# First feed-forward of a hybrid attention and mLSTM network: output projection token-major with 512 weight columns, results transposed by TensorE

## The chip, the cores and the metric

One core of one Trainium2 chip runs the whole program. The metric is the device time of one execution in microseconds; the number of a kernel is the median of its runs. The engines are TensorE (PE: matmuls, with the weight loads PEld on a path of their own), VectorE (DVE), ScalarE (ACT), GpSimd (POOL) and SyncE (SP, which issues most DMAs). PE reads its operands from SBUF and writes PSUM, which has eight banks of 128 partitions by 512 fp32 columns.

## The reference

A network of two layers, 512 tokens, width 1024, feed-forward width 2816, all fp32:

```python
def swiglu(xn, w_in, w_out):
    gu = xn @ w_in
    return (jax.nn.silu(gu[..., :D_FF]) * gu[..., D_FF:]) @ w_out
...
    h = x
    for i in range(DEPTH):
        j = i // N_MIXERS
        if i % N_MIXERS == 0:
            h = h + dilated_attention_mixer(rms_norm(h, attn_norm[j]), positions,
                                            attn_w_in[j], attn_w_out[j])
        else:
            h = h + mlstm_mixer(rms_norm(h, mlstm_norm[j]), mlstm_w_in[j], mlstm_conv_w[j],
                                mlstm_conv_b[j], mlstm_ig_bias[j], mlstm_fg_bias[j],
                                mlstm_head_gain[j], mlstm_w_out[j])
        h = h + swiglu(rms_norm(h, ffn_norm[i]), ffn_w_in[i], ffn_w_out[i])
    return rms_norm(h, final_norm)
```

So the order is: attention, feed-forward 0, mLSTM, feed-forward 1, final norm. The change touches the last product of feed-forward 0 (`@ w_out`), the addition to `h`, and the norm and the first projection of the mLSTM mixer behind it.

## The kernel before

The residual `h` is held feature-major: eight tiles of 128 features by 512 tokens (`h0` to `h7`, after feed-forward 0 `hn0` to `hn7`). Every fp32 product is made as three products of rounded parts, hi·hi, hi·lo and lo·hi (`SPLITS`); a value is split by ACT (the high part, `_h`) and DVE (the rest, `_l`). A weight chunk is 128 partitions by 1024 fp32 values (512 KB), loaded by SP, and split by L210 (ACT) and L211 (DVE).

*The output projection* (`output_products`, L1371) multiplies 2816 hidden features by 1024 outputs for 512 tokens. Twenty of the 22 hidden chunks go through a Strassen-Winograd scheme with 2x2 blocks: token halves by hidden halves by output halves. That gives seven products P1 to P7, each in five units of 256 hidden features (`UNITS`), 35 unit-products in all; the last two chunks ("rest") are multiplied plainly, in two column halves `first` and `second`. A list written by hand (`order`, L1560) fixes the sequence; each item's weights and operands are prepared two items ahead (`AHEAD`). The last three items, P4_3, P4_4 and second_0 (`TAIL`), are not run in that order but tile by tile, so that the results become ready one after the other.

The two feed-forwards run it in two forms. In feed-forward 0 (`sums_of_rows` true) the weights are stationary, in blocks of 128x128, and 256 tokens move: `tile_mm` (L1609 to L1619), 24 matmuls of 256 columns to a unit-product. The results come out feature-major. P5's weights are sums of rows that are loaded apart (`load_first_sum`: ten loads by SP, ten more by POOL that add in flight, tiles `f0S`). Half results are copied from bank to bank by ACT (`copy_half`, L1635) and added to `h` by DVE (`add_sum`, L1640). In feed-forward 1 the activations are stationary and 512 weight columns move (L2023, L2089): 12 matmuls of 512 columns to a unit-product. Its results come out token-major, which the final output wants.

*The seam into the mLSTM.* `natural` (L1629, DVE) adds a finished bank to the old `h` and permutes the tokens, giving `hn`. `norm` (L1094) then splits each of the eight `hn` into `n_h` (ACT, L228) and `n_l` (DVE, L229) and sums their squares (`n2sq` by ACT, L380, `n2ssum` by DVE, L381). The sums over features are four small matmuls (`n2ss`, L1109), which are deferred: they are issued inside the projection of the first value columns (`project_tokens_wide`, L320, tiles `mv0`), behind the tile that `amid` names, before `(1, 1)`: the second chunk's second token block. DVE takes the reciprocal root from there (L1111, L340, L190 to L195), builds eight diagonal blocks (`n2dg`, L349), and PE spreads them over the partitions (`n2bc`, L355) after the gates' matmuls (L1730); DVE copies that to `n2rbc` (L356). The gate rows and everything behind the first q and k projection (`mqk`, L241) use it.

Each engine runs its instructions in the program's order as a scheduler laid it out; `issue_after` and `defer` move single pieces within that order.

Of the kernel before, what the change touches and what calls it, by code (L numbers as in the profile page):

```python
# [17 lines left out]
P = 128  # L18
# [54 lines left out]
def tile_hybrid_dilated_attn_mlstm(  # L73
# [1020 lines left out]
    def norm(key, k0, name, ssum=None, wait=1):  # L1094
        pair = x_tiles(name)
        add = None
        if ssum is None:
            ssum, add = squares_of(name)
        for k in range(KC):
            split_act(pair[0][k], pair[1][k], h[k], col(key, k0 + k))  # L1100
            if add is not None:
                add(k)
        v = npl.tile([P, TB], F32, tag="rs_v4", name=name + "v", bufs=2)
        box = {}

        def sums():
            sp = ps.tile([P, 512], F32, tag="t", name=name + "ss", bufs=1)
            for tb in range(TB):
                nc.tensor.matmul(sp[:, tb:tb + 1], ssum[:, tb * P:(tb + 1) * P], ones[:, 0:1],  # L1109
                                 start=True, stop=True)  # L1110
            nc.vector.tensor_copy(v, sp[:, :TB])  # L1111
# [259 lines left out]
    def output_products(layer, fp, wo, sums_of_rows):  # L1371
# [11 lines left out]
        ROWS = ({"P2": (1, 0), "P7": (1, 1), "P4": (1, 1)} if sums_of_rows else  # L1383
                {"P2": (1, 0), "P7": (0, 0), "P3": (1, 1)})
# [23 lines left out]
        first_sums = {}  # L1408

        def load_first_sum(u):  # L1410

            src = [weight_rows(hk * UNITS + u, 1) for hk in range(2)]
            place = (((npl, "sq", 2),) * 2, ((npl, "rbc", 1), (fp, "gu0", 3)), ((fp, "u2", 1), (fp, "v5", 1)),
                     ((fp, "gu1", 2),) * 2, ((fp, "gu0", 3),) * 2)[u]
            parts = [(p.tile([P, 1, 512], F32, tag=tg, name="f%dS1_%d" % (layer, u), bufs=bufs), slice(k, k + 1))
                     for k, (p, tg, bufs) in enumerate(place)]
            for t, ks in parts:
                nc.sync.dma_start(t, src[0][:, ks])
                nc.gpsimd.dma_start(t, src[1][:, ks], accum_op=ALU.add)  # L1419
            first_sums[u] = parts  # L1420

        def prepare_first_sum(u, own, nm):

            view = lambda t: t.rearrange("p (k n) -> p k n", k=2)
            hi = wp.tile([P, 1024], F32R, tag="whi", name=nm + "_h", bufs=W_BUFS)
            lo = wp.tile([P, 1024], F32R, tag="wlo", name=nm + "_l", bufs=W_BUFS)
            for t, ks in first_sums[u]:
                nc.scalar.activation(view(hi)[:, ks], t, AF.Copy)
                subtract(view(lo)[:, ks], t, view(hi)[:, ks].bitcast(F32))
            whl["P5", u] = view(hi), view(lo)  # L1430
            for t, ks in first_sums[u]:
                subtract(view(own)[:, ks], t, view(own)[:, ks])
            split_operand("P5", u, sums[u])

        def prepare_product(name, u):
# [21 lines left out]
            in_place = ("P1", "P6", "P3") if sums_of_rows else ("P1", "P5", "P6", "P4")  # L1457
            if sums_of_rows and name == "P5":
                prepare_first_sum(u, t, nm)
                return  # L1460
            raw = t if name in in_place else load(*ROWS[name])
            if sums_of_rows:

                if name == "P7":
                    nc.vector.tensor_tensor(raw, raw, t, op=ALU.add)
                    add_rows(t, 1, 0)


            elif name == "P7":
# [3 lines left out]
            if sums_of_rows and name == "P1":  # L1473

                for i in {0: (0,), 1: (1,), UNITS - 1: range(2, UNITS)}.get(u, ()):
                    load_first_sum(i)
            if sums_of_rows:
                if name == "P6":
                    negate(t)
            elif name in ("P1", "P5"):  # L1480
# [15 lines left out]
            elif name == "P6":  # L1496
                split_operand(name, u, half(u, 1))
                if sums_of_rows:
                    subtract(sums[u], half(u, 1), half(u, 0))
            elif name == "P7":  # L1500
                split_operand(name, u, sums[u])
            elif name == "P3":
                if not sums_of_rows:
                    subtract(half(u, 1), half(UNITS + u, 0), half(u, 1))
                split_operand(name, u, half(UNITS + u, 1) if sums_of_rows else half(u, 1))
            elif name == "P4":
                if sums_of_rows:
                    subtract(half(UNITS + u, 0), half(UNITS + u, 0), half(u, 1))
                split_operand(name, u, half(UNITS + u, 0 if sums_of_rows else 1))

        def prepare_rest(n, pi):
# [9 lines left out]
            if sums_of_rows and n == second:  # L1521

                view = lambda t: t.rearrange("p (k n) -> p k n", k=2)
                raw = fp.tile([P, 1024], F32, tag="t1", name=nm + "_w")
                nc.sync.dma_start(view(raw), weight_rows(pi, n))
                t = fp.tile([P, 2, 1024], F32R, tag="w8", name=nm + "_hl", bufs=2)
                hi, lo = t[:, 0], t[:, 1]
                nc.scalar.activation(hi, raw, AF.Copy)
                subtract(lo, raw, hi.bitcast(F32))
                whl[n, pi] = view(hi), view(lo)  # L1530
            elif n == second:
# [10 lines left out]
        def during(j, i):  # L1542
            u = j // 2 - (FC // 2 - UNITS)
            if i == 1 and 0 <= u < UNITS:
                p, tag, bufs = (fp, "sums", UNITS - 1) if u < UNITS - 1 else (npl, "ssum", 1)
                sums.append(p.tile([P, 2, HALF], F32, tag=tag, name="f%dS%d" % (layer, u), bufs=bufs))
                if sums_of_rows:
                    subtract(sums[u], half(u, 1), half(u, 0))
                else:
                    nc.vector.tensor_tensor(sums[u], half(u, 1), half(UNITS + u, 1), op=ALU.add)  # L1550
            if i == 4 and 0 <= u < UNITS:
                subtract(half(u, 1), *((half(UNITS + u, 1), sums[u]) if sums_of_rows else (sums[u], half(u, 0))))
# [24 lines left out]
        def work(product, plain, then):  # L1577

            for i, (kind, *key) in enumerate(items[:-TAIL]):
                prepare(i + AHEAD)  # L1580
                key = tuple(key)
                if not sums_of_rows and key == ("P7", UNITS - 1):
# [8 lines left out]
            for i in range(len(items) - TAIL + AHEAD, len(items) - (not sums_of_rows)):  # L1591
# [4 lines left out]

    pair, rbc, _, hook = norm("ffn", 0, "n1", ssum)
    with ExitStack() as fctx:
        fp = pool(fctx, "ffn0")
        hid, during, prepare, work = output_products(0, fp, ffn_w_out[0], True)  # L1600
# [3 lines left out]
        F = [[ps.tile([P, 512], F32, tag=tag, name="fo%d" % n, bufs=3 if tag == "acc" else 2 - (tag == "t"))  # L1604
              for tag in tags] for n, tags in enumerate((("s", "s", "acc", "acc"), ("o", "o", "acc", "t")))]
        ts = [slice(0, HALF), slice(HALF, SEQ)]
        target = {"P1": (0, 0), "P2": (0, 0), "P5": (0, 1), "P3": (0, 1), "P6": (1, 0), "P7": (1, 0), "P4": (1, 0)}

        def tile_mm(acc, m, b, w, fresh=False):  # L1609
            for k in range(2):  # L1610
                for a_, b_ in SPLITS:
                    nc.tensor.matmul(acc, w[a_][:, k, m * P:(m + 1) * P], b[b_][k],
                                     start=(fresh and k == 0 and (a_, b_) == SPLITS[0]),
                                     stop=(k == 1 and (a_, b_) == SPLITS[-1]), skip_group_check=True)

        def product(name, u, b, w):
            n, t = target[name]
            for m in range(4):
                tile_mm(F[n][m][:, ts[t]], m, b, w, name == "P1" and u == 0)  # L1619

        def plain(n, pi, b, w):
            for m in range(4):
                tile_mm(F[n][m], m, b, w)

        old, h = h, []
# [7 lines left out]
        def copy_half(t):  # L1633
            for m in range(4):
                nc.scalar.activation(F[1][m][:, ts[t]], F[0][m][:, ts[t]], AF.Copy)  # L1635

        def add_sum(n):
            for m in range(4):
                o = old[4 * n + m][:, ts[1]]
                nc.vector.tensor_tensor(o, F[1][m][:, ts[0]], o, op=ALU.add)  # L1640

        def first_tiles():
            for m in range(4):
                natural(m, F[0][m])
        last = work(product, plain, {("P1", 4): lambda: copy_half(0), ("P5", 4): lambda: copy_half(1),
                                     ("P6", 4): lambda: add_sum(0), ("P7", 4): lambda: add_sum(1)})
        first_tiles()

# [492 lines left out]
```

## Time and profile before

| | us |
|---|---|
| median of 3 runs | 1397.77 (1396.92 to 1398.39) |
| the profiled execution | 1398.66 |
| its span | 1396.7 |
| PE busy | 1380.6 |
| DVE busy | 1120.2 |
| ACT busy | 703.0 |
| POOL busy | 153.7 |

The span is the time between the first and the last instruction of the profiled execution, on which all times of the trace lie. An engine's busy time counts the time in which it had an instruction under way; matmuls overlap, so that a matmul's own duration in the trace is longer than the distance to the next one, and the pace is read from starts.

### The profile page before, as it was taken

What the parts mean: (1) busy time and instruction counts of PE and PEld (TensorE: products, weight loads), DVE (VectorE), ACT (ScalarE), POOL (GpSimd) and SP (SyncE); (2) the same over time, 40 slices, a digit from 0 to 9 for tenths busy, and PEclk for the clock granted to TensorE, in tenths of its full rate; (3) what the DMA queues carried; (4) which work ended last, traced back from release to release, by engine and by line L of the source; (5) the groups of instructions that cost most, each with busy time, mean ns of one, the idle gap of its engine ahead of it and who ended that gap; (6) DMA issues with size and microseconds to landing.
All of it is one profiled execution on the core that took longest, in us unless ns stands there. A gap on an engine that the chain in (4) does not pass through costs nothing. (4 is left out here: it accounts for less than half of the span.)

```text
span 1396.7 us, 21529 instructions
## 1 busy us (share of the span) xinstructions
PE 1380.6 (99%) x8308; PEld 1232.4 (88%) x8308; DVE 1120.2 (80%) x1904; ACT 703.0 (50%) x1153; POOL 153.7 (11%) x223
## 2 busy tenths in 40 slices
PE   9999999999999999999999999999999999999997
PEld 7888888888888788999999998888888899999886
DVE  7978769695868299877877898898858987887877
ACT  5335552222324155445566464786534544458854
POOL 1000011111010000000010100113201240001213
PEclk9999999999999999999999999999999999999999
DMA  7534256346363446333253643324334563335963
GB/s 228 164 121 136 76 166 190 120 138 195 96 191 92 157 145 158 121 122 115 92 164 85 154 134 92 92 77 106 95 117 116 134 196 121 122 104 133 198 162 106
DMA packets 136830, 186.00 MB, mean 133 GB/s; under 512 B 8532, under 2 KB 104340, under 8 KB 136728
## 3 DMA queue, kind: packets, MB, share of 16 engines
q1 hardware_dynamic: 117600, 136.14, 30.5%
q0 software_dynamic: 17472, 47.37, 14.7%
q8 instruction: 65, 1.06, 0.3%
q10 hardware_dynamic: 1656, 1.12, 0.2%
q14 instruction: 37, 0.30, 0.1%
HBM read 163.63 MB, written 18.87 MB: 131 GB/s over the span
## 5 line engine op out<-in xcount | busy, mean ns | idle before, releaser
L1444 POOL DMA_DIRECT2D f1T<-in_ffn_w_out_dram x15 | 17.8, 1186 | 207.5 <-DMA f1P_2w_w<-in_ffn_w_out_dram 136.0
L1419 POOL DMA_DIRECT2D f0S<-in_ffn_w_out_dram x10 | 8.8, 919 | 256.7 <-DMA f0S<-in_ffn_w_out_dram 189.6
L1976 POOL DMA_DIRECT2D hD<-hB x32 | 21.7, 697 | 68.5 <-DVE hB L1973 68.2
L241 PE MATMUL mo<-n_h,mo_k_l 128*128 128x512 f32 x64 | 25.3, 396 | 0.0
L241 PE MATMUL mo<-n_h,mo_k_h 128*128 128x512 f32 x64 | 25.2, 394 | 0.0
L241 PE MATMUL mo<-n_l,mo_k_h 128*128 128x512 f32 x64 | 25.2, 393 | 0.0
L241 PE MATMUL mqk<-n_h,mqk_k_h 128*128 128x512 f32 x64 | 25.1, 393 | 0.0
L241 PE MATMUL mwo<-yo_l,mwo_k_h 128*128 128x512 f32 x64 | 25.1, 392 | 0.0
L241 PE MATMUL awo<-ao_h,awo_k_h 128*128 128x512 f32 x64 | 25.1, 392 | 0.0
L241 PE MATMUL mqk<-n_l,mqk_k_h 128*128 128x512 f32 x64 | 25.1, 392 | 0.0
L241 PE MATMUL f0j<-n_h,f0j_h 128*128 128x512 f32 x64 | 25.0, 391 | 0.0
L241 PE MATMUL f1j<-n_h,f1j_h 128*128 128x512 f32 x64 | 25.0, 391 | 0.0
L241 PE MATMUL mwo<-yo_h,mwo_k_l 128*128 128x512 f32 x64 | 25.0, 391 | 0.0
L241 PE MATMUL mqk<-n_h,mqk_k_l 128*128 128x512 f32 x64 | 25.0, 390 | 0.0
L241 PE MATMUL awo<-ao_h,awo_k_l 128*128 128x512 f32 x64 | 24.9, 390 | 0.0
L241 PE MATMUL f0j<-n_h,f0j_l 128*128 128x512 f32 x64 | 24.9, 390 | 0.0
L241 PE MATMUL f1j<-n_h,f1j_l 128*128 128x512 f32 x64 | 24.9, 390 | 0.0
L241 PE MATMUL awo<-ao_l,awo_k_h 128*128 128x512 f32 x64 | 24.9, 389 | 0.0
L241 PE MATMUL f0j<-n_l,f0j_h 128*128 128x512 f32 x64 | 24.9, 389 | 0.0
L241 PE MATMUL f1j<-n_l,f1j_h 128*128 128x512 f32 x64 | 24.9, 389 | 0.0
L241 PE MATMUL mwo<-yo_h,mwo_k_h 128*128 128x512 f32 x64 | 24.8, 391 | 0.0
L211 DVE TENSOR_TENSOR v1P_l<-v1W,v1P_h 128x1024 fp32r<-128x1024 f32 x14 | 17.1, 1223 | 9.6 <-ACT v1P_h L210 9.6
(2491 smaller groups left out, 5671.1 us busy)
## 6 DMA issues: line engine op xcount, KB each, us to landing
f0j_w<-in_ffn_w_in_dram SPq DMA_DIRECT2D x17, 512.0 KB, 6.0
f1j_w<-in_ffn_w_in_dram SPq DMA_DIRECT2D x17, 512.0 KB, 5.4
f1T<-in_ffn_w_out_dram POOLq DMA_DIRECT2D x15, 512.0 KB, 6.7
f0hid<-in_ffn_w_in_dram SPq DMA_DIRECT2D x9, 512.0 KB, 5.5
f1hid<-in_ffn_w_in_dram SPq DMA_DIRECT2D x9, 512.0 KB, 5.0
v0W<-in_attn_w_in_dram SPq DMA_DIRECT2D x8, 512.0 KB, 6.0
v1W<-in_attn_w_in_dram SPq DMA_DIRECT2D x8, 512.0 KB, 4.0
awo_k_w<-in_attn_w_out_dram SPq DMA_DIRECT2D x8, 512.0 KB, 4.0
```

The lines of the kernel that those rows point to most:

```text
L211: nc.vector.tensor_tensor(lo[:, :n], raw[:, :n], hi[:, :n].bitcast(F32), op=ALU.subtract)
L241: nc.tensor.matmul(acc, whl[a][:, k, m * P:(m + 1) * P], pairs[b][kk], start=(kk == 0 and (a, b) == SPLITS[0]), stop=(kk == nk - 1 and (a, ...
L1419: nc.gpsimd.dma_start(t, src[1][:, ks], accum_op=ALU.add)
L1444: nc.gpsimd.dma_start(view(to), weight_rows(hk * UNITS + u, n), accum_op=ALU.add)
L1976: nc.gpsimd.dma_start(hD[k // 4].rearrange("(b i) x -> i b x", i=R)[:, :, c0:c0 + R], t[R * a_:R * (a_ + 1)])
```

## The change

Feed-forward 0 takes the form of feed-forward 1. The helpers that were feed-forward 1's own move into `output_banks`, which both use. `first_columns=1` exchanges the column halves, so that the half that is finished first holds features 0 to 511. The results are kept token-major in SBUF (`rows_of`, in the hidden tiles that are free by then): ACT copies banks out (`keep_banks`), DVE adds banks (`add_banks`). `features` transposes a column half back, sixteen 128x128 blocks by TensorE into four banks, from which `natural` adds to the old `h` as before. The first half's transposes stand behind tail tile tb 2. The second half's, with the splits and squares of its four features, are deferred (`late`) into the first value chunk, which now stands within feed-forward 0's pool; the deferred work is issued behind that chunk's second tile (`amid` (0, 1)), and the tail's tiles run in the order 2, 3, 0, 1.

```diff
-    def norm(key, k0, name, ssum=None, wait=1):
+    def norm(key, k0, name, ssum=None, wait=1, late=None):
...
-        for k in range(KC):
-            split_act(pair[0][k], pair[1][k], h[k], col(key, k0 + k))
-            if add is not None:
-                add(k)
+
+        def take(ks):
+            for k in ks:
+                split_act(pair[0][k], pair[1][k], h[k], col(key, k0 + k))
+                if add is not None:
+                    add(k)
+        take(range(len(h)))
+        if late is not None:
+            defer(1, lambda n=len(h): (late(), take(range(n, KC))))
...
-        ROWS = ({"P2": (1, 0), "P7": (1, 1), "P4": (1, 1)} if sums_of_rows else
-                {"P2": (1, 0), "P7": (0, 0), "P3": (1, 1)})
+        ROWS = {"P2": (1, 0), "P7": (0, 0), "P3": (1, 1)}
...
         def weight_rows(pi, n):
+            n ^= first_columns
...
-            for t, ks in parts:
-                nc.sync.dma_start(t, src[0][:, ks])
-                nc.gpsimd.dma_start(t, src[1][:, ks], accum_op=ALU.add)
...
-        first, second = (0, 1) if sums_of_rows else (1, 0)
-        order = ("P1_0 P1_1 P1_2 P1_3 P1_4 P5_0 P2_0 P5_1 P2_1 P6_0 P5_2 P2_2 P6_1 P5_3 P2_3 P6_2 P5_4 P2_4 P6_3 P6_4 "
-                 "P7_0 first_0 P7_1 P7_2 P3_0 P7_3 P3_1 P7_4 P3_2 P3_3 P4_0 P3_4 P4_1 P4_2 P4_3 P4_4 second_0"
-                 if sums_of_rows else
+        first, second = 1, 0
+        order = (
                  "P1_0 P1_1 P1_2 P1_3 P1_4 P5_0 P2_0 P5_1 P2_1 P5_2 P2_2 P5_3 P2_3 P5_4 P2_4 P6_0 P3_0 P6_1 P3_1 P6_2 P3_2 "
                  "P6_3 P3_3 P6_4 P3_4 P7_0 P7_1 first_0 P7_2 P4_0 P7_3 P4_1 P7_4 P4_2 P4_3 P4_4 second_0").split()
...
+        def multiply_half(acc, a, t, w, fresh=False):
+
+            for m in range(2):
+                for k in range(2):
+                    for a_, b_ in SPLITS:
+                        nc.tensor.matmul(acc[m], a[a_][k][:, (2 * t + m) * P:(2 * t + m + 1) * P], w[b_][:, k, :],
+                                         start=(fresh and k == 0 and (a_, b_) == SPLITS[0]),
+                                         stop=(k == 1 and (a_, b_) == SPLITS[-1]), skip_group_check=True)
...
-        hid, during, prepare, work = output_products(0, fp, ffn_w_out[0], True)
+        hid, during, prepare, work = output_products(0, fp, ffn_w_out[0], 1)
...
-        def tile_mm(acc, m, b, w, fresh=False):
-            for k in range(2):
-                for a_, b_ in SPLITS:
-                    nc.tensor.matmul(acc, w[a_][:, k, m * P:(m + 1) * P], b[b_][k],
...
+        rows_of = {(tb, n): hid[3 * n + tb // 2][:, tb % 2] for tb in range(TB) for n in range(2)}
+
+        def keep_banks(tbs, src, n):
+            copy_banks([rows_of[tb, n] for tb in tbs], src)
+
+        def add_banks(tbs, src, n):
+            for m, tb in enumerate(tbs):
+                nc.vector.tensor_tensor(rows_of[tb, n], src[m], rows_of[tb, n], op=ALU.add)
+
+        def plain(n, pi, a, w):
+            for t in range(2):
+                multiply_half((p5, c22)[t], a, t, w)
+            add_banks((0, 1), p5, 1)
+            keep_banks((2, 3), c22, 1)
+
+        def after_p7():
+            add_banks((2, 3), u_, 1)
+            keep_banks((2, 3), u_, 0)
...
+        def features(n):
+
+            tps = []
             for m in range(4):
-                nc.scalar.activation(F[1][m][:, ts[t]], F[0][m][:, ts[t]], AF.Copy)
-
-        def add_sum(n):
+                tp = bank("t" if m == 3 else "acc", "T%d" % (4 * (1 - n) + m))
+                for tb in range(TB):
+                    transpose_into(tp, tb, rows_of[tb, n][:, m * P:(m + 1) * P])
+                tps.append(tp)
             for m in range(4):
-                o = old[4 * n + m][:, ts[1]]
-                nc.vector.tensor_tensor(o, F[1][m][:, ts[0]], o, op=ALU.add)
-
-        def first_tiles():
-            for m in range(4):
-                natural(m, F[0][m])
...
+                natural(4 * (1 - n) + m, tps[m])
...
-        for m in range(4):
-            for kind, b, w in last:
-                tile_mm(F[1][m][:, ts[0]] if kind == "product" else F[1][m], m, b, w)
-            natural(4 + m, F[1][m])
+        p4 = target["P4"]
+        for tb in (2, 3, 0, 1):
+            acc = c11[tb] if tb < 2 else p4[tb - 2]
+            run(lambda: tile_of(last, acc, tb))
+            if tb < 2:
+                nc.scalar.activation(rows_of[tb, 0], acc, AF.Copy)
+            else:
+                add_banks((tb,), (acc,), 0)
+            if tb == 2:
+                run(lambda: features(1))
+            if tb == 3:
+                ready = [wide_chunk(values, 0, "mv0")]
         ready.append(wide_chunk(values, 1, "mv0"))
...
-    pair, rbc, rtok, hook = norm("mlstm", 0, "n2", wait=2)
+        pair, rbc, rtok, hook = norm("mlstm", 0, "n2", wait=2, late=lambda: features(0))
+        wide = [ps.tile([P, 512], F32, tag=tag, name="mv0", bufs=2) for tag in "soso"]
+        project_tokens_wide(pair, values, wide, None, "mv0", (0,), ready, (0, 1))
...
-        base = tick[0]
-
-        wide = [ps.tile([P, 512], F32, tag=tag, name="mv0", bufs=2) for tag in "soso"]
+        base = tick[0] - 1
...
-            project_tokens_wide(pair, values, wide, evac_wide, "mv0", chunks, ready, (1, 1))
-        first_values((0, 1))
+            project_tokens_wide(pair, values, wide, evac_wide, "mv0", chunks, ready)
+        first_values((1,))
```

More of the change, by code (lines that the diff above doesn't have):

```diff
@@ L1456, in prepare_product @@
             t = tw[u]
[L1457 to L1469, printed above, removed]
+            raw = load(*ROWS[name]) if name in ROWS else t
+            if name == "P7":
                 nc.vector.tensor_tensor(raw, raw, t, op=ALU.add)
@@ L1472, in prepare_product @@
             whl[name, u] = split_chunk((raw, 1024, view, nm))
[L1473 to L1480, printed above, removed]
+            if name in ("P1", "P5"):
                 negate(t)
@@ L1520, in prepare_rest @@
             nm = "f%dw%d_%d" % (layer, n, pi)
[L1521 to L1531, printed above, removed]
+            if n == second:
                 raw, _, view, _ = load_chunk(weight_rows(pi, n), [P, 2, 512], nm)
@@ L1642, in first_tiles @@
-        def first_tiles():
-            for m in range(4):
-                natural(m, F[0][m])
-        last = work(product, plain, {("P1", 4): lambda: copy_half(0), ("P5", 4): lambda: copy_half(1),
-                                     ("P6", 4): lambda: add_sum(0), ("P7", 4): lambda: add_sum(1)})
-        first_tiles()
+                natural(4 * (1 - n) + m, tps[m])
+        last = work(product, plain, {("P1", 4): lambda: copy_banks(u_, c11), ("P5", 4): lambda: copy_banks(c22, p5),
+                                     ("P6", 4): lambda: keep_banks((0, 1), u_, 1), ("P7", 4): after_p7})
@@ L2079, in tile_hybrid_dilated_attn_mlstm @@
         for acc, tb, cs in tiles:
-            todo = [e for e in last if tb >= 2 or e[0] == "rest"]
-            def block_of():
-                for i, (kind, a, w) in enumerate(todo):
-                    block = tb - 2 if kind == "product" else tb
-                    for k in range(2):
-                        for a_, b_ in SPLITS:
-                            wk = w[b_][k] if kind == "rest" else w[b_][:, k]
-                            nc.tensor.matmul(acc[:, cs], a[a_][k][:, block * P:(block + 1) * P], wk[:, cs],
-                                             start=(acc is rest_of and i == 0 and k == 0 and (a_, b_) == SPLITS[0]),
-                                             stop=(i == len(todo) - 1 and k == 1 and (a_, b_) == SPLITS[-1]),
-                                             skip_group_check=True)
-            run(block_of)
+            run(lambda: tile_of(last, acc, tb, cs, acc is rest_of))
             output(tb, 0, acc, 2 if cs.stop == 512 else 1, cs)
```

105 lines of the change are left out of this document (36 added, 69 removed).

## The prediction, made before the changed kernel ran

> **What bounds the kernel now.** I read the page first: engine shares, the granted clock, the chain that ended last.
>
> ```profile
> PE 1380.6 (99%) x8308; PEld 1232.4 (88%) x8308; DVE 1120.2 (80%) x1904; ACT 703.0 (50%) x1153; POOL 153.7 (11%) x223
> PEclk9999999999999999999999999999999999999999
> PE 30%; DVE 6%; ACT 2%; issue 1%; ACTq 0%; DVEq 0%
> ```
>
> TensorE (PE) works 99% of the span at full clock; VectorE (DVE) is the only other engine in the chain for more than 2%. The stretches around the change come from the view of windows (PE, weight loads, DVE, ACT, POOL, clock, DMA):
>
> ```profile
> 725.62:820.90 95.28, 95.28 (x775) 94.32 (x774) 78.22 (x103) 55.81 (x77) 10.37 (x10) 1.00 0.51 128
> 820.90:846.50 25.60, 25.60 (x162) 23.17 (x162) 24.52 (x34) 15.23 (x23) 3.68 (x13) 1.00 0.38 106
> 853.60:902.60 49.00, 48.63 (x271) 41.99 (x270) 47.45 (x88) 31.71 (x50) 4.44 (x4) 1.00 0.31 94
> 887.00:1013.00 126.00, 123.93 (x728) 107.47 (x728) 108.00 (x299) 88.39 (x217) 27.80 (x36) 1.00 0.35 95
> ```
>
> The output projection (from 725.62) has no PE gap, so there a matmul saved is time saved. But at its end DVE is busy 24.52 of 25.60 us, then 47.45 of 49.00: at this seam into the mLSTM, and for 50 us behind it, DVE is nearly as tight as PE.
>
> **What is removed, added and moved.** *Products.* 840 matmuls of 256 columns become 420 of 512; the 48 of the two rest halves had 512 already. Paces are start to start in the timelines, 24 old matmuls between the first two rows, 12 new ones between the next two:
>
> ```profile
> 725.62 0.40 PE L1612 MATMUL fo<-f0P,f0P_0w_h 128*128 128x256 f32 x2
> 728.50 0.40 PE L1612 MATMUL fo<-f0P,f0P_1w_h 128*128 128x256 f32 x2
> 1285.17 0.39 PE L2023 MATMUL finc<-f1P_1w_h,f1P 128*128 128x512 f32 x1
> 1287.89 0.39 PE L2023 MATMUL finc<-f1P_2w_h,f1P 128*128 128x512 f32 x1
> L1612 PE MATMUL fo<-f0P,f0P_0w_h 128*128 128x256 f32 x112 | 20.4, 283 | 0.0
> L1612 PE MATMUL fo<-f0P,f0P_0w_l 128*128 128x256 f32 x56 | 15.8, 283 | 0.0
> ```
>
> (112 + 56) x 5 units = 840. A unit-product took 2.88 us and takes 2.72: 35 x 0.16 = **-5.6 us**. Per matmul that is 0.120 against 0.227 us.
>
> The Trainium skill, page "TensorE: Matmul & The Clock Gate", section "Back-to-back issue gap", gives N/2.4 + 2.5 ns for the isolated gap at full clock; by it 840 x 109.2 - 420 x 215.8 ns is an estimate of only 1.1 us saved, which speaks against the change. The rows differ: 120 and 227 ns are measured here, some 11 ns over the rule in either form, which the narrow form pays twice as often, and the sum keeps 5.6.
>
> *Transposes.* The results now stand tokens by features and the residual is feature-major: 32 transposes of 128x128, in two runs of 16. The input's transposes use the same helper:
>
> ```profile
> 11.62 0.39 PE L497 MATMUL a0g0q<-xa_h,first_l 128*128 128x512 f32 x1
> 11.85 1.91 PE L331 MATMUL xT<-cst,x_tok 128*128 128x128 f32 x16
> 14.58 0.40 PE L497 MATMUL a0g0q<-xa_h,first_h 128*128 128x512 f32 x1
> 16.43 0.39 PE L497 MATMUL a0g0q<-xa_h,first_l 128*128 128x512 f32 x1
> 16.66 1.03 PE L331 MATMUL xT<-cst,x_tok 128*128 128x128 f32 x8
> 18.00 0.39 PE L497 MATMUL a0g0q<-xa_h,first_l 128*128 128x512 f32 x1
> L331 PE MATMUL xT<-cst,x_tok x32: 270/272/361, 6.3 to 17.4; 128*128 128x128 f32 x32
> 11.85:13.51 1.66, 1.66 (x17) 1.66 (x16) 0.71 (x3) 1.02 (x2) 1.41 (x5) 1.00 1.07 362
> ```
>
> From 11.62 to 14.58 lie 16 transposes and four matmuls: 2.96 - 4 x 0.23 = 2.04 us with the switches. From 16.43 to 18.00, 8 and three: 0.89, so 16 cost 1.78. I take 1.9 a run, **+3.8 us**, bounds 3.6 and 4.1. PE net is **-1.8** (-2.0 to -1.5). The transposes' weight loads and matmuls both stand on PE's queue and nothing can hide them: PE has no gap there.
>
> The same page, "Part 4: PE-mode transpose", puts a 128x128 transpose at about 275 ns in a kernel and says the full clock doesn't engage for them. The 272 ns median agrees as a duration, but 16 of them began within 1.66 us at a granted clock of 1.00: they overlap. The rule, taken as a pace, is the fourth rival.
>
> *Work off PE.* Gone are ten SP loads and ten accumulating POOL loads (f0S, the summed weights of P5), in their place ten more accumulating loads in place (five before, fifteen in the last feed-forward). ACT copies twelve 128x512 banks in place of eight half copies (L1635); DVE adds six 512-wide banks in place of eight half adds (L1640).
>
> ```profile
> L1419 POOL DMA_DIRECT2D f0S<-in_ffn_w_out_dram x10 | 8.8, 919 | 256.7 <-DMA f0S<-in_ffn_w_out_dram 189.6
> f1T<-in_ffn_w_out_dram POOLq DMA_DIRECT2D x15, 512.0 KB, 6.7
> L1635 ACT ACTIVATE fo<-fo x8: 365/368/377, 738.2 to 775.3; 128x256 f32<-128x256 f32 x8
> L2050 ACT ACTIVATE finu<-finc x2: 576/576/576, 1295.2 to 1296.7; 128x512 f32<-128x512 f32 x2
> L1640 DVE TENSOR_TENSOR h<-fo,h x8: 415/422/425, 781.3 to 809.0; 128x256 f32<-128x256 f32 x8
> L2054 DVE TENSOR_TENSOR ht<-finu,ht x6: 681/684/686, 1347.4 to 1377.2; 128x512 f32<-128x512 f32 x6
> 1282.42:1381.00 98.58, 98.58 (x437) 81.64 (x436) 81.74 (x102) 68.58 (x90) 21.59 (x18) 1.00 0.71 158
> ```
>
> ACT: 12 x 0.58 - 8 x 0.37 = +4.0 us, DVE: 6 x 0.68 - 8 x 0.42 = +0.7. Both I cost at nothing up to the tail: the last feed-forward runs the same order, the same fifteen loads on POOL and the same copies, and its PE is busy 98.58 of 98.58 us. Without that cover a late load (6.7 us) would show as PE idle, up to a few us.
>
> *The seam.* Here cover is thin. Before, four of the eight residual adds (natural, L1629) stood ahead of the tail and the rest between its tiles; now all eight wait for transposes. By the paces: the tail starts at 725.62 + 33 x 2.72 + 24 x 0.227 = 820.8; tile tb 2 (18 matmuls) ends at 824.9, the first 16 transposes at 826.8, tb 3 at 830.9, tb 0 and 1 (six each) at 833.6, two value tiles at 836.3, the second 16 transposes at 838.2, and the remaining 36 value matmuls bring PE to the sums n2ss at 846.4.
>
> ```profile
> 845.57 0.95 PE L1109 MATMUL n2ss<-ones,n2ssum 128*128 128x1 f32 x8
> 852.88 0.62 PE L355 MATMUL n2bc<-n2dg,ones_r 128*128 128x512 f32 x2
> 864.24 0.39 PE L241 MATMUL mqk<-n_h,mqk_k_h 128*128 128x512 f32 x1
> 839.84 1.06 DVE L1629 TENSOR_TENSOR hn<-fo,h 128x512 f32<-128x512 f32 x1
> 840.74 0.68 DVE L381 TENSOR_TENSOR n2ssum<-n2ssum,n2sq 128x512 f32<-128x512 f32 x1
> 841.34 0.74 DVE L229 SCALAR_TENSOR_TENSOR n_l<-hn,cols,n_h 128x512 fp32r<-128x512 f32 x1
> 842.00 0.68 DVE L381 TENSOR_TENSOR n2ssum<-n2ssum,n2sq 128x512 f32<-128x512 f32 x1
> 846.55 0.16 DVE L1111 COPY n2v<-n2ss 128x4 f32<-128x4 f32 x1 [1.13 <-PE n2ss L1109]
> L211 DVE TENSOR_TENSOR mv_k_l<-mv_k_w,mv_k_h 128x1024 fp32r<-128x1024 f32 x4 | 4.9, 1219 | 0.0
> 850.99 1.22 DVE L211 TENSOR_TENSOR mv_k_l<-mv_k_w,mv_k_h 128x1024 fp32r<-128x1024 f32 x1
> 853.54 0.69 DVE L356 COPY n2rbc<-n2bc 128x512 f32<-128x512 f32 x1 [1.33 <-PE n2bc L355]
> ```
>
> For the late four features DVE needs, start to start, four adds at 0.90, four splits n_l at 0.66 and four sums at 0.60: 8.6 us. The first late group of four transposes is done near 837, so the last sum ends near 846: about 0.4 us before PE wants it. n2ss stands 0.8 later than before with 12 more value matmuls behind it. DVE then runs its reciprocal root (846.55 to 850.99: 4.4 us) with one value-weight split (1.22) now ordered into it; the diagonals are ready near 853.2. In the changed order PE has sixteen gate matmuls and seven of values for that time, with n2ss 0.95 + 23 x 0.227 = 6.2 us, so it is done at 852.6 and waits about 0.6 us at n2bc. Queued behind that wait are the two of n2bc, 41 value matmuls, then mqk: 853.2 + 43 x 0.227 = 863.0 instead of 864.24. So 0.5 to 0.6 of the 1.8 is lost, and **-1.2 to -1.3 us** is left. Behind it, DVE's copy n2rbc comes about where it did, but the first mqk weight split, which followed it at once, is now done ahead, and one more has moved behind the first head's decay matrix: DVE gains 1.22 less the 0.4 us by which n2rbc comes later, 0.8 us, up to 2.0 with the second: about PE's shift, which I let through.
>
> **Sum.** -5.6 + 3.8 + 0.5 = **-1.3 us**. The profiled execution took 1398.66 us (span 1396.7), 0.89 above the median 1397.77: 1397.4 on its terms, **1396.5** as a median.
>
> **Rivals.** *1, more comes through: 3 to 5 us.* PE's waits in the mLSTM hang on DVE's order:
>
> ```profile
> 907.25 1.16 DVE L1868 SCALAR_TENSOR_TENSOR m1e<-m1s,m1e 128x512 f32<-128x512 f32 x2 [2.34 <-PE m1s L1867]
> ```
>
> Between 887 and 1013 PE is idle 126.00 - 123.93 = 2.1 us; an earlier DVE there could remove it, with -1.8 on PE about -3.9: 1393.9. Against it: DVE is 108.00 of 126.00 busy there and one such wait can come back elsewhere. The end of it is transposes at no cost, -5.6, which the full PE rules out.
>
> *2, slower: DVE late at the seam.* One place, n2ss: PE waits as soon as DVE is over 0.4 us late. The price is what DVE work stands ahead of the late adds: four splits of value weights lie in this stretch (the group of 4.9 us); if two of them come before the late features, PE waits 2.4 - 0.4 at n2ss and 0.6 at n2bc, -1.8 + 2.6 = +0.8; if all four, +3.3 (1401.1). For it: DVE is at 96% there. Against it: DVE had 1.13 and 1.33 us idle at exactly these two places. I put the case at +2.
>
> *3, nothing: DVE sets the pace from 853 on,* so that what PE gains before is given back by 925; 1397.8. For it: 47.45 of 49.00. Against it: DVE's idle 2.34 us before m1e is a wait for PE.
>
> *4, the transposes don't overlap.* 32 x 0.272 = 8.7 instead of 3.8: -5.6 + 8.7 = +3.1, 1400.9. The 1.66 us for 16 speak against it. (The pace is that of the rule in the Trainium skill, "TensorE: Matmul & The Clock Gate", "Part 4: PE-mode transpose".)
>
> **How the numbers follow.** Forecast 0.42; more 0.24; DVE late 0.25; nothing 0.07; serial transposes 0.02. About 0.2% (2.8 us) is what a measurement tells from no change: faster than 1395.0 is the case of more and a little of the forecast, 0.27; slower than 1400.6 the upper part of DVE late, the serial transposes and some of the uncovered loads, 0.19; within, 0.54. The likeliest one's own range is 1395.5 to 1397.8; for 8 in 10 it reaches from 1393.4, below the 1393.9 of the first rival, to 1401.1, all four splits.
>
> **What would show it.** In the changed profile: unit-products 2.72 us apart and no PE idle from 725.6 to the tail; each run of 16 transposes near 1.9 us; the tail starting near 821; n2ss near 846.4 without a wait, a short one at n2bc; mqk near 863. A PE wait over 1 us at n2ss, or m1s later than before, makes the slower case; an end over 3 us earlier than mqk's shift makes the first rival.

## The result: slower, with the loss in front of the tail

| | us |
|---|---|
| before, median of 5 runs | 1398.05 (1396.92 to 1399.02) |
| changed, median of 5 runs | 1403.33 (1402.35 to 1404.62) |
| ratio | 1.0036, interval 1.0025 to 1.0048 |
| span of the profiled execution | 1396.7 before, 1401.2 after |

The forecast was 1396.5. The page of the changed kernel shows PE's busy time (engine, us, share, instructions):

```profile
PE 1380.0 (98%) x7920; PEld 1213.1 (87%) x7920; DVE 1116.0 (80%) x1888; ACT 714.1 (51%) x1163; POOL 156.1 (11%) x223
```

388 matmuls fewer, and 4.5 us more span. The view of waits, PE in the stretch 700 to 900, names what PE stood for (total, times, longest):

```profile
PE fou L1550 <- ACT f0P_3w_h L210: 1.4, 1, 1.4
PE fou L1550 <- DVE f0P_3w_l L211: 0.8, 1, 0.8
PE mv L320 <- ACT f0hid L1630: 0.7, 1, 0.7
PE n2bc L355 <- DVE n2dg L349: 0.3, 1, 0.3
```

The first two stand in the products: P7_3 waits for its split weights. The last feed-forward of the kernel before, whose form the change copies (the template, from here on), has no such wait. The timeline of PE gives the milestones: first product, first matmul of the tail, the transposes, first value tile, sums, first q/k matmul, first output matmul of the mLSTM:

```profile
725.81 0.40 PE L1550 MATMUL foc<-f0P_0w_h,f0P 128*128 128x512 f32 x1
824.17 0.39 PE L1571 MATMUL fop<-f0P_3w_h,f0P 128*128 128x512 f32 x1
828.02 0.39 PE L1571 MATMUL fop<-f0w_h,f0hl 128*128 128x512 f32 x1
828.26 1.91 PE L331 MATMUL foT<-cst,f0hid 128*128 128x128 f32 x16
830.24 0.40 PE L1571 MATMUL fop<-f0P_3w_l,f0P 128*128 128x512 f32 x1
837.69 0.50 PE L320 MATMUL mv<-mv_k_h,n_h 128*128 128x512 f32 x1 [0.71 <-ACT f0hid L1630]
850.50 1.02 PE L1114 MATMUL n2ss<-ones,n2ssum 128*128 128x1 f32 x8
867.10 0.39 PE L241 MATMUL mqk<-n_h,mqk_k_h 128*128 128x512 f32 x1
1014.41 0.39 PE L241 MATMUL mwo<-yo_h,mwo_k_h 128*128 128x512 f32 x1
```

From the first product to the tail are 98.4 us where 33 x 2.72 + 24 x 0.227 = 95.2 were due. In the kernel before it was 826.12 - 725.62 = 100.5; its tail begins here:

```profile
826.12 0.40 PE L1612 MATMUL fo<-f0P,f0P_3w_h 128*128 128x256 f32 x2
```

The transposes cost what was said, or a little less: from 828.02 to 830.24 lie sixteen of them and two matmuls, 2.22 - 0.45 = 1.77 us a run.

Why P7_3's weights were late is in ACT's timeline, with the matching stretch of the last feed-forward of the kernel before behind it:

```profile
809.53 0.63 ACT L1482 ACTIVATE f0w_h<-f0w_w 128x512 fp32r<-128x512 f32 x1 [5.71 <-DMA f0w_w<-in_ffn_w_out_dram]
810.07 1.06 ACT L1556 ACTIVATE f0hid<-foc 128x512 f32<-128x512 f32 x2
811.02 1.06 ACT L210 ACTIVATE f0P_3w_h<-f0P_3w_w 128x1024 fp32r<-128x1024 f32 x1
```

```profile
1363.37 0.63 ACT L1537 ACTIVATE f1w_h<-f1w_w 128x512 fp32r<-128x512 f32 x1 [2.62 <-DMA f1w_w<-in_ffn_w_out_dram]
1363.91 1.04 ACT L210 ACTIVATE f1P_3w_h<-f1P_3w_w 128x1024 fp32r<-128x1024 f32 x1
```

At the head of ACT's queue stands the split of the second rest half's weights, needed only in the tail. ACT waits 5.71 us for their load, against 2.62 in the template, and the split starts 83.7 us after the first product, against 1363.37 - 1282.42 = 81.0; the bank copies and P7_3's split are queued behind. The loads in front were late as well. The timeline of VectorE, POOL and SP of the changed kernel (the sum of P7_1's weight rows, the accumulating load that follows it, the loads of the first rest half and of P7_2), and the row of P7_2's load in the DMA view of 784 to 812 (KB, us to landing); behind them the same for the last feed-forward of the kernel before (1340.6 to 1368.6):

```profile
789.12 1.23 DVE L1437 TENSOR_TENSOR f0P_1w_w<-f0P_1w_w,f0T 128x1024 f32<-128x1024 f32 x1 [2.77 <-DMA f0P_1w_w<-in_ffn_w_out_dram]
790.89 1.20 POOL L1422 DMA_DIRECT2D f0T<-in_ffn_w_out_dram  x1 [5.68 <-ACT f0hid L1556]
791.51 0.37 SPq L202 DMA_DIRECT2D f0w_w<-in_ffn_w_out_dram  x1
792.65 0.37 SPq L202 DMA_DIRECT2D f0P_2w_w<-in_ffn_w_out_dram  x1
```

```profile
f0P_2w_w<-in_ffn_w_out_dram SPq DMA_DIRECT2D x1, 512.0 KB, 7.7
```

```profile
1347.56 0.37 SPq L202 DMA_DIRECT2D f1P_2w_w<-in_ffn_w_out_dram  x1
1350.39 1.18 POOL L1444 DMA_DIRECT2D f1T<-in_ffn_w_out_dram  x1 [8.27 <-DVE f1P_1w_w L1470]
```

```profile
f1P_2w_w<-in_ffn_w_out_dram SPq DMA_DIRECT2D x1, 512.0 KB, 4.5
```

The sum ended at 790.35; the releaser named with POOL's issue is the event nearest ahead of it in time, a copy that it does not need. In the template the accumulating load of P7_1 starts 2.8 us after P7_2's load, in the changed kernel 1.8 us ahead of it, and P7_2's takes 7.7 us in place of 4.5. What held it back in the template was VectorE: there the finished banks of P6 are added on VectorE, and P7_1's sum, which releases the accumulating load, is queued behind those adds. In the changed kernel ACT copies these banks out, and the sum runs earlier. That this order is the cause is what the experiments have to show.

### The profile page after: what moved, and what is told of

Its sections match the earlier page's. It is cut to its first block, busy times and chain, and to the rows that moved or that the text cites. A ratio compares the mean times of both kernels' runs of the same rounds, so it can differ in the third digit from the quotient of the medians.

```text
span 1401.2 us, 20723 instructions
## 1 busy us (share of the span) xinstructions
PE 1380.0 (98%) x7920; PEld 1213.1 (87%) x7920; DVE 1116.0 (80%) x1888; ACT 714.1 (51%) x1163; POOL 156.1 (11%) x223
## 5 line engine op out<-in xcount | busy, mean ns | idle before, releaser
L1422 POOL DMA_DIRECT2D f0T<-in_ffn_w_out_dram x15 | 17.9, 1228 | 259.8 <-DMA f0P_2w_w<-in_ffn_w_out_dram 189.9
L241 PE MATMUL mo<-n_h,mo_k_l 128*128 128x512 f32 x64 | 25.3, 396 | 0.0
```

Of the source, the lines that this page charges most:

```text
L241: nc.tensor.matmul(acc, whl[a][:, k, m * P:(m + 1) * P], pairs[b][kk], start=(kk == 0 and (a, b) == SPLITS[0]), stop=(kk == nk - 1 and (a, ...
L1422: nc.gpsimd.dma_start(view(to), weight_rows(hk * UNITS + u, n), accum_op=ALU.add)
```

## The experiments

Unless said otherwise each is one edit on the changed kernel. An edge is one more rule of order: an instruction may not be issued before another one. Behind each median stands its ratio to the kernel before, measured in the same round, with its 95% interval; as that kernel's median moved from 1398.05 to 1399.34 us between rounds, kernels of different rounds are compared by these ratios. "Products" is the time from the first product to the first tail matmul, from PE's timeline as above.

**The order on VectorE.** An edge lets P7_1's sum start only after P3_4's split:

```diff
+        split_at = {}
...
-                nc.vector.tensor_tensor(raw, raw, t, op=ALU.add)
+                with tc.issue_after(split_at["P3", 4]) if layer == 0 and u == 1 else nullcontext():
+                    nc.vector.tensor_tensor(raw, raw, t, op=ALU.add)
...
+            split_at[name, u] = last_on(mybir.EngineType.DVE)
```

> The changed kernel with one edge more on VectorE: the sum of P7_1's two weight rows may not start before the split of P3_4's weights. Theory A (a wait on VectorE in the wrong place): in the changed kernel that sum stands ahead of P3_4's split and waits 2.8 us for its load; the split frees the buffer for the next load, so every load behind it is some 2 us late, ACT then waits 5.7 us for the second rest half's weights and TensorE 2.2 us (3.2 with the restarts) for P7_3's. With the edge the sum's wait holds up nothing: the first rest weights are loaded at most 66.0 us after the stage's start instead of 65.7 + 2, TensorE's waits in the products shrink from 2.2 to under 0.7 us, n2ss comes 2.5 to 3.2 us earlier, and the kernel takes 1400.0 to 1401.0 us instead of 1403.3. Theory B (ACT's queue is too full by the bank copies, whatever VectorE's order): no change, 1403 us, the wait for P7_3 stays over 1.5 us. Theory C (the seam and the transposes, not the products, made the loss): no change over 0.5 us.

It took 1405.52 us, ratio 1.0051 (1.0034 to 1.0068): slower still. The edge did what it should to the first load, which is issued 63.7 us after the first product in place of 65.7, but P7_2's now took 8.9 us to land, and the products 825.28 - 724.24 = 101.0 us. A late issue was not the cause; theory A fell, and the loads themselves came into question. The edge had not moved the accumulating load of P7_1 behind P7_2's load: it still starts 0.6 us ahead of it (789.59 and 790.23).

**The second rest half later.** Its preparation is called behind the last P4's.

> The changed kernel with the split of the last rest half's weights (the 5.7 us wait of ACT) issued behind the splits of the last P4 weights instead of behind P7_4. Theory A: the weights of P7_3 are there when ACT comes free, so this takes away the last link of the same chain: TensorE's wait for P7_3 falls from 2.2 to under 0.7 us though the loads stay late; but the rest half's split then comes near its use in the tail and may cost up to 1 us there; 1400.0 to 1402.0 us. Theory B: the same gain, 3 us, 1400.3 us. Theory C: no change, 1403 us. A and B are told apart by the run with the edge on VectorE: A has both gain, B only this one.

1403.63 us, 1.0035 (1.0023 to 1.0047), no change. The edit missed: only one of the two parts of the split moved, and ACT's wait for the load stayed at 6.0 us. It says nothing on the theory.

**The copies at the seam first.**

```diff
                 if add is not None:
-                    add(k)
+                    with tc.issue_after(after[0]) if after and k == 3 else nullcontext():
+                        add(k)
...
                 nc.scalar.activation(rows_of[tb, 0], acc, AF.Copy)
+                copied[:] = [last_on(mybir.EngineType.Activation)]
```

> The changed kernel with one edge more on ACT: the square of the fourth early feature may not start before the copies of the tail's last two banks. In the changed kernel that square waits 1.2 us for VectorE and the copies queue behind it; TensorE waits 0.7 us (1.1 with its restart) for the first value tile. All theories on the products leave them as they are: waits of 2.2 us there. If the wait at the seam reaches the end, n2ss comes 0.8 to 1.0 earlier and the kernel takes 1402.4; if VectorE's late features set n2ss anyway, n2ss moves by less than 0.3 and the time stays at 1403.3.

1402.50 us, 1.0026 (1.0015 to 1.0037). The wait before the first value tile is gone. The ratio's interval overlaps that of the changed kernel, and the products happened to be slower in the profiled execution (825.08 - 725.06 = 100.0 us; why is told in the last section), so the seam is read from the tail's start: to n2ss 25.3 us (825.08, 850.40) in place of 26.3 (824.17, 850.50), and to the first mwo matmul 189.2 (1014.29) in place of 190.2 (1014.41). One us is won, and in these two profiles it reaches the output projection whole.

**The transposes twice.**

```diff
                 for tb in range(TB):
-                    transpose_into(tp, tb, rows_of[tb, n][:, m * P:(m + 1) * P])
+                    for _ in range(2):
+                        transpose_into(tp, tb, rows_of[tb, n][:, m * P:(m + 1) * P])
```

> The changed kernel with every one of the 32 transposes issued twice, the second over the first. It measures their price. As overlapped work at the pace of the trace (16 in 1.77 us) they add 3.5 us on TensorE, and as nothing can hide them there n2ss comes 3.5 later: 1406.9 us. If they don't overlap (0.272 us each) they add 8.7: 1412. If what sets the end is VectorE's late features and not TensorE, the second run is partly hidden and the time rises by 1.8 to 2.5.

1407.35 us, 1.0062 (1.0047 to 1.0077), by the ratios 0.26% or 3.6 us over the changed kernel; products 825.61 - 725.09 = 100.5. From the tail's start to n2ss it takes 2.5 us more, as the 1 us of the wait at the seam is filled. 2.5 + 1.0 is the 3.5 of work that overlaps; serial transposes, 8.7, are excluded. The run of transposes itself shows it: 3.65 us for 32, where 16 took 1.91.

```profile
829.69 3.65 PE L331 MATMUL foT<-cst,f0hid 128*128 128x128 f32 x32
```

**P6's banks on VectorE, and P7_1's sum later.** The first restores the template's order on VectorE; the second moves only the sum, behind P7_0's split, with the edge of the first experiment and `split_at["P7", 0]` in it.

```diff
+        def keep_p6():
+            for m in range(2):
+                nc.vector.tensor_copy(rows_of[m, 1], u_[m])
...
-                                     ("P6", 4): lambda: keep_banks((0, 1), u_, 1), ("P7", 4): after_p7})
+                                     ("P6", 4): lambda: keep_p6(), ("P7", 4): after_p7})
```

> The changed kernel with P6's two finished banks copied out by VectorE instead of ACT, at the same place. That puts VectorE's order as in the last feed-forward: the sum of P7_1's weight rows, and with it the accumulating load that follows it, comes after these copies, about 2.5 us later. Theory D (the DMA engines): in the changed kernel that accumulating load starts ahead of the loads for the first rest half, P7_2 and P7_3 and runs beside them; P7_2's load then takes 7.7 us instead of 4.5 in the last feed-forward, and all that follows is late. Then P7_2's load lands in under 6.5 us here, the wait of ACT for the last rest weights falls from 5.7 to under 4, the products take 95.2 to 96.5 us instead of 98.4 to 101, and the kernel 1399.5 to 1401. Theory B (ACT's queue): ACT has two copies less, 1.1 us, so the wait shrinks by about 1 us, to 1402. If neither, 1403.3.

> The changed kernel with one edge: P7_1's sum of weight rows on VectorE waits until P7_0's split is done, so that the accumulating load behind it starts about 1.5 to 2 us later and the loads of the first rest half and P7_2 are issued ahead of it; ACT keeps its copies. Theory D: P7_2's load lands in under 6.5 us, the products take under 97 us and the kernel 1400 to 1401.5. Theory B: no change, 1403. If the loads come too close in any order (the DMA engines are simply full), P7_2's load gets faster and another one slower, and the products stay at 98 to 101 us.

1400.43 us, 1.0008 (0.9998 to 1.0017), and 1400.76 us, 1.0011 (1.0001 to 1.0021). P7_2's load landed in 4.9 and 6.0 us, as the accumulating load now starts 2.8 and 1.6 us behind it (both timelines, SP and POOL):

```profile
791.27 0.37 SPq L202 DMA_DIRECT2D f0P_2w_w<-in_ffn_w_out_dram  x1
794.11 1.20 POOL L1422 DMA_DIRECT2D f0T<-in_ffn_w_out_dram  x1 [8.62 <-DVE f0P_1w_w L1437]
```

```profile
789.29 0.37 SPq L202 DMA_DIRECT2D f0P_2w_w<-in_ffn_w_out_dram  x1
790.92 1.20 POOL L1423 DMA_DIRECT2D f0T<-in_ffn_w_out_dram  x1 [7.59 <-ACT f0P L1406]
```

The products took 821.88 - 726.13 = 95.8 and 820.38 - 724.01 = 96.4 us. With ACT's copies in place the second still wins most of it: what matters is when the accumulating load starts. The length of ACT's wait is no measure of it: in the second ACT waits even 6.96 us for the rest half's weights, but this wait ends 81.7 us after the first product in place of 83.7.

**Without the accumulating loads behind P7.**

```diff
                 nc.vector.tensor_tensor(raw, raw, t, op=ALU.add)
-                add_rows(t, 1, 0)
+                if layer == 1:
+                    add_rows(t, 1, 0)
```

> The changed kernel without the five accumulating loads behind P7 in the first feed-forward: P4's weights lack one of their summands. It takes 2.5 MB of accumulating transfer from the DMA engines in the last third of the products and leaves every instruction of PE, ACT and VectorE where it was. Theory D and a full DMA in general: no wait of TensorE in the products, 95.2 to 95.6 us for them, and the kernel 1399.5 to 1400.5. Theory B: the second rest half's split still heads ACT's queue, but its load no longer comes late, so no telling apart from D here; if the waits stay over 1.5 us, neither the DMA engines nor the loads are the cause.

1399.83 us, 1.0005 (0.9995 to 1.0014); products 819.44 - 724.21 = 95.2, no wait. P7_2's load lands in 5.0 us here, though P7_3's starts only 2.1 us behind it. So it is the accumulating transfers, and not the plain loads beside them, that cost the stall; the order of PE's, ACT's and VectorE's instructions was left as it was.

**ACT's queue.** The second rest half's split is held behind P7_4's, this time both parts:

```diff
+            split_at[name, u] = last_on(mybir.EngineType.Activation)
...
                 for k in range(2):
-                    nc.scalar.activation(parts[0][k], view(raw)[:, k], AF.Copy)
+                    with tc.issue_after(split_at["P7", 4]) if layer == 0 else nullcontext():
+                        nc.scalar.activation(parts[0][k], view(raw)[:, k], AF.Copy)
```

> The changed kernel with the second rest half's split held behind P7_4's split on ACT: the earlier try had left one of its two parts at the head of the queue. Theory B (what stalls TensorE is that ACT's queue stands 5.7 us behind a weight that is needed only in the tail): P7_3's split runs at once, TensorE's wait for it falls from 2.2 to 2.6 us to under 0.8, the products take 95.2 to 96.5, the kernel 1399.8 to 1401. If P7_3's own weights are late (theory D without the queue), the wait stays over 1.5 us.

1400.33 us, 1.0008 (0.9999 to 1.0018); products 821.60 - 725.63 = 96.0. P7_2's load is as slow as in the changed kernel (the DMA view, 782 to 812), yet ACT's timeline has the bank copies and P7_3's split early:

```profile
f0P_2w_w<-in_ffn_w_out_dram SPq DMA_DIRECT2D x1, 512.0 KB, 7.8
```

```profile
803.48 0.60 ACT L1559 ACTIVATE f0hid<-foc 128x512 f32<-128x512 f32 x1
804.84 0.60 ACT L1559 ACTIVATE f0hid<-foc 128x512 f32<-128x512 f32 x1 [0.76 <-PE foc L1553]
807.36 1.06 ACT L210 ACTIVATE f0P_3w_h<-f0P_3w_w 128x1024 fp32r<-128x1024 f32 x1 [1.92 <-DVE f0P_3w_w L1438]
```

So it takes two links to stall PE: loads that crowd each other, and an ACT queue that waits for the least urgent of them first. Taking away either brings the products from 98.4 to between 95.8 and 96.4 us in these profiles; by the ratios, 1.0036 against 1.0008 to 1.0011, it is worth 3.5 to 4 us, with an interval of more than 1 us either way.

**All three mends together**: P6 on VectorE, the rest half held on ACT, the copies first.

> The changed kernel with three of the edits together: P6's banks copied out by VectorE, the second rest half's split held behind P7_4's on ACT, and the square of the fourth early feature behind the copies of the tail's last two banks. Theory (queues and loads made the loss): products 95.2 to 95.6 us without a wait, no wait before the first value tile, n2ss 120.5 to 121 us after the stage's start, the stage's lead over the kernel before at the last heads 0.6 to 0.8 us, and 1398.5 against 1399.3 of before. If the transposes and VectorE's work behind them cost more than the products save, it stays at 1400 or above.

1398.55 us against 1399.14, 0.9997 (0.9989 to 1.0006): level with before. Its timeline (first product, tail, n2ss, VectorE's n2v, mqk, a wait at the first heads, mwo) and a row of its windows:

```profile
725.65 0.40 PE L1554 MATMUL foc<-f0P_0w_h,f0P 128*128 128x512 f32 x1
820.88 0.39 PE L1575 MATMUL fop<-f0P_3w_h,f0P 128*128 128x512 f32 x1
846.21 1.02 PE L1115 MATMUL n2ss<-ones,n2ssum 128*128 128x1 f32 x8
847.40 0.14 DVE L1117 COPY n2v<-n2ss 128x4 f32<-128x4 f32 x1
862.81 0.39 PE L241 MATMUL mqk<-n_h,mqk_k_h 128*128 128x512 f32 x1
900.27 0.38 PE L1857 MATMUL m0s<-qs,ks 128*128 128x256 f32 x1 [0.65 <-DVE m0e L1859]
1010.04 0.39 PE L241 MATMUL mwo<-yo_h,mwo_k_h 128*128 128x512 f32 x1
```

```profile
847.00:897.00 50.00, 49.60 (x273) 42.60 (x273) 48.47 (x105) 28.38 (x39) 1.33 (x2) 1.00 0.29 85
```

This is the schedule that was predicted: n2ss 846.2 (846.4), n2v 847.4, mqk 862.8 (863.0), 1.4 us ahead of the kernel before. At the output projection 0.7 us of it is left; before, that row reads:

```profile
1010.74 0.39 PE L241 MATMUL mwo<-yo_h,mwo_k_h 128*128 128x512 f32 x1
```

About half is lost at the first heads, where PE waits 0.65 us for VectorE, which is busy 48.47 of the 50 us ahead. VectorE's m0e, which PE waits for, starts only 0.3 us earlier than before (first row with the mends, second row before):

```profile
899.54 1.14 DVE L1859 SCALAR_TENSOR_TENSOR m0e<-m0s,m0e 128x512 f32<-128x512 f32 x2
899.85 1.15 DVE L1868 SCALAR_TENSOR_TENSOR m0e<-m0s,m0e 128x512 f32<-128x512 f32 x2
```

**A split out of the root's chain.** All three mends, and the last value chunk's weight split behind the diagonals.

> The run with all three edits, and one edge more: the last value chunk's weight split (1.2 us on VectorE), which stands inside the chain of the reciprocal root, comes behind the diagonals. TensorE's wait at n2bc (0.4 us) goes, and the copy n2rbc comes 1.1 to 1.2 us earlier. If VectorE sets the pace from there to the first heads (it is busy 43.0 of 44.0 us), the first heads come 0.8 to 1.2 us earlier at m0s; 1397.6. If TensorE sets it, only the 0.4 to 0.6 us of its wait are won; 1398.1. If the split is merely as late again behind, nothing.

1398.08 us, 0.9995 (0.9986 to 1.0003). VectorE's copy n2rbc comes at 853.10 in place of 853.97, but the wait at m0s stays at 0.63 us and mwo begins at 1010.32, no earlier. Moving this work within VectorE's queue wins nothing: the view of waits lists none of VectorE's between n2ss and the heads, and the same work is due before m0e. That speaks for VectorE as the limit there; a run with less work on it was not made.

**The last feed-forward too**, and, for an even comparison, the same edit on the kernel before.

> The run before this one, and in the last feed-forward too the second rest half's split held behind P7_4's on ACT: its TensorE waited 0 to 1.2 us for P7_3 in the profiles so far, in the same place and by the same chain as the first feed-forward's. Expected: no wait there, the end 0.3 to 1.2 us earlier; 1397.0. If those waits come from the loads themselves and not from ACT's queue, no change.

> The kernel before, with the one edit of the last run that doesn't belong to the change: in the last feed-forward the second rest half's split is held behind P7_4's on ACT. It makes the comparison even. If the last feed-forward's waits are in part what spreads the runs of the kernel before (1397.0 to 1400.6), this takes 1398.2 to 1398.8 against 1399.2, and the changed form with all its mends (1397.1) is then 1.1 to 1.7 us ahead of it, near the 0.7 us that the profiles show at the last heads. If the kernel before never waited there, no change, and the mended form is 2 us ahead.

1397.11 us against 1399.14, 0.9986 (0.9977 to 0.9995), and 1397.27 against 1398.83, 0.9987 (0.9978 to 0.9996). Holding the rest half's split back in the last feed-forward is a gain of 0.13% on the kernel before. On the changed form, 0.9986 against 0.9995 of the run ahead, the intervals overlap, and the gain is not told from nothing. Why it helps is not shown: in the profile of the kernel before PE has no wait in that feed-forward, and from its first matmul to its last it takes 1388.64 - 1282.42 = 106.2 us, and 1387.79 - 1281.58 = 106.2 with the split held back. With it in both, the mended change is not told from the kernel before.

## Why the prediction was wrong, by its own steps

- *Products, -5.6 us*: right. The paces hold, and with all three mends the products take 95.2 us where the kernel before took 100.5; the other 0.3 belongs to the two unit-products in the tail.
- *Transposes, +3.8*: right, 3.5 measured, so PE's net was -2.1. The fourth rival, serial transposes, is out.
- *Work off PE, costed at nothing "up to the tail"*: the step that failed. It reasoned that "the last feed-forward runs the same order, the same fifteen loads on POOL and the same copies" and has no PE gap. The order of the list is the same, but not the engines: of the twelve bank copies that it counts for ACT the template has four. ACT, not VectorE, takes P6's banks out, and VectorE's adds had spaced the loads. The stall cost 3.2 us in the profile (98.4 for 95.2). In two others with the same product code (the copies first, the transposes twice) the products lost 4.8 and 5.3, of which 1.7 each was a lower clock behind the wait (last section). The step's own fallback, a late load "would show as PE idle, up to a few us", gives the right size, but the prediction took it to be covered and let only "some of the uncovered loads" into its 0.19 for a slower end.
- *The seam*: the arithmetic was right to 0.2 us once the queues were mended, but it left out that PE's first value tile needs a bank which ACT copies out, and that ACT stands behind a square that waits for VectorE. That cost 1.0 us.
- *VectorE late at n2ss* (second rival): wrong place. PE never waited at n2ss. At n2bc it waited 0.3 us in the changed kernel and 0.4 with all three mends; 0.6 was forecast.
- *"About PE's shift, which I let through"*: half right. VectorE was to gain 0.8 us and up to 2.0; its m0e starts 0.3 us earlier. Of 1.4 us at mqk 0.7 arrive. The third rival, VectorE's pace from 853 on, takes the other half, as far as the profiles tell; it was not tested.

Together, at the first matmul of the output projection: -0.7, what all mends leave, + 3.2 for the stall, + 1.0 for the seam, + 0.2 as the stage began later (725.81 for 725.62) is 3.7, and mwo moved by 1014.41 - 1010.74 = 3.7. The other 0.8 of the span's 4.5 us lies behind PE's work: PE has no wait in the last feed-forward of this profile, and its last matmul, at 1392.36 in place of 1388.64, is still 3.7 late. From there to the issue of the last store (1397.29 in place of 1393.14) 0.4 us more are lost, and as much until the end; why was not traced.

## What to carry to other kernels

A stage that runs without gaps is a template only with the same engines in the same places: an operation that seems merely to take time on one engine may be what spaces the transfers behind it. In an engine's in-order queue a split that waits for a load belongs behind the splits that are needed sooner, however early its own load was issued. And a saving on the busiest engine is worth what the next engine can follow: here 2.1 us of PE time became 0.7 at the next output projection.

## What the runs showed of the hardware

An accumulating load takes about twice the engine time of a plain one. In the stretch 784 to 812 of the changed kernel the DMA view gives (queue, packets, MB, share of the 16 engines' time):

```profile
q0 software_dynamic: 939, 1.82, 39.1%
q1 hardware_dynamic: 1632, 3.15, 34.8%
```

28 us x 0.391 / 1.82 = 6.0 us of all 16 engines to a MB on POOL's queue, which here carries the accumulating loads, against 3.1 on SP's. SP's plain loads took 28 x 0.420 / 3.67 = 3.2 in the run without the accumulating loads behind P7 (same stretch), so theirs is no price of running beside the others; accumulating loads alone were not measured.

The same product code took 98.4, 100.0 and 100.5 us in three profiles. PE's waits for P7_3 explain a small part of that: 2.2, 2.6 and 2.8 us. Most of the rest is the granted clock behind them. The view of windows, 814 to 817, of the changed kernel, of the copies first and of the second rest half later (PE, weight loads, DVE, ACT, POOL, clock, DMA):

```profile
814.00:817.00 3.00, 3.00 (x15) 2.48 (x14) 3.00 (x5) 1.28 (x2) 0.00 (x0) 1.00 1.08 267
814.00:817.00 3.00, 3.00 (x9) 2.35 (x8) 3.00 (x4) 0.20 (x1) 0.00 (x0) 0.50 0.91 255
814.00:817.00 3.00, 3.00 (x14) 2.42 (x14) 3.00 (x5) 0.72 (x2) 0.00 (x0) 1.00 1.11 257
```

At a granted clock of 0.50 the view has 9 matmuls where it has 15 at 1.00. Taken by single microseconds, what the clock lacks to 1.00 from 813 to 818 adds up to 0.08 + 0.50 + 0.50 + 0.50 + 0.12 = 1.7 us in the second row's execution. It is 1.7 too with the transposes twice, and with the order on VectorE, where PE waits 3.7 us. So a stall cost 1.7 us more in these, in a stretch where PE counts as busy for 3.00 of 3.00 us. What decides it is not shown: the third row's execution waited 2.6 us, as long as the second's, and kept its clock.
